# Mixer stage of a two-layer decoder trunk: its loads in one queue in order of use, no subtractions on GpSimd, another order of the first dense products

## The chip, the core and the metric

One core of a Trainium2 chip runs the whole trunk in one launch. The metric is the device time in microseconds of one execution. An execution is also profiled: its trace gives every instruction of the five engines (TensorE or PE with its weight loads PEld, VectorE or DVE, ScalarE or ACT, GpSimd or POOL, SyncE or SP), every DMA transfer, and the clock that TensorE was granted.

## What is computed

Two layers over 256 tokens of width 1024. Layer 0 is a causal pooling mixer and a dense SwiGLU, layer 1 a sparse attention and eight SwiGLU experts of which each token takes two. Each sub-layer ends in LayerNorm(ALPHA * x + f(x)). The change lies in the mixer and at the start of the dense layer:

```python
def pool_mixer(x, w_grp, scale):
    # four groups of 256 channels, windows 2, 4, 8, 16: running mean over the window, minus x
    ...
    y = jnp.einsum('bsgc,gcd->bsgd', pooled - xg, w_grp).reshape(B, S, D_MODEL)
    return y * scale

def swiglu(x, w_gu, w_down):
    g, u = jnp.split(x @ w_gu, 2, axis=-1)
    return (jax.nn.silu(g) * u) @ w_down

# layer 0
x = layer_norm(ALPHA * x + pool_mixer(x, pool_w, pool_scale), ln_g[0, 0], ln_b[0, 0])
x = layer_norm(ALPHA * x + swiglu(x, ffn_w_gu, ffn_w_down), ln_g[0, 1], ln_b[0, 1])
```

## The kernel before

**Numbers in two parts.** A float32 factor of the dense layer and of the attention's projections is split into a high part (ScalarE, a copy that rounds, line 154 for weights, 297 for activations) and a low part (VectorE or GpSimd, the difference, lines 164 and 300). A product is three matmuls: high by high, low by high, high by low. Weights come in units of 128 x 2048 floats (1 MB), in a fixed list; class `Units` walks it: `fetch` issues the DMA on SP's queue into one of four raw buffers (line 145) and the high copy, `low` makes the low part of the oldest unit that lacks it, on GpSimd if `pool=True`, and `take` hands out the pair. A raw buffer is free again when its low part is made.

**Mixer.** x lies as two halves of 128 tokens, `x0[:, 0]` and `x0[:, 1]`. `pooled(t, q)` multiplies x by constant window matrices `pc` (lines 398 and 400; the second half of the tokens needs both halves of x), ScalarE copies the result to `pT` (401), `mixed(t)` multiplies by the group weights `pw` into the banks `py` (407). VectorE scales `pw` by `pool_scale` (`scl`) first (413). `layer_norm` then runs on VectorE: per quarter of the channels a scaled sum and its statistics (240, 241), small steps on 128 x 1 values (254 to 263) with the two centrings by the gain among them (245), and the final scaling with the bias (277). TensorE transposes the result by the identity, which lies in `keep` (294), ScalarE takes the high part `xH`, VectorE the low part `xL`. The low parts of all four pieces are made after both halves are normalised (`lows`).

**What sets the order.** Every engine runs its instructions in the order in which the program writes them; the tile framework puts in the waits. SP's queue carries x, the matrices, `pw` and the weight units; GpSimd's queue carries `scl`, gain and bias `ln`, `keep` and `cst` (constants that the attention uses first). The first two weight units get their low parts from GpSimd, written behind the mixing and inside the loop over the halves; the third from VectorE behind the `lows`.

**First dense product.** `gate_up(0, ...)` (lines 440 to 461) multiplies unit 0 in three passes over 2 x 8 matmuls (447): high weights by `xH`, low weights by `xH`, high weights by `xL`. Its gate part `pg` stands in one of two banks with the tag `gu`, which the transposes of the second half of the tokens used last; its up part `pu` in one of four with the tag `acc`. Later products do the three matmuls in turn (223 to 225).

**After the front.** The dense layer has 22 such products and 11 down products, then the attention, then per expert 28 units of gate and up weights and 14 of down weights, whose DMAs run ahead as far as the raw buffers allow.

Of the kernel before, what the change touches and what calls it, by code (L numbers as in the profile page):

```python
# [12 lines left out]
BF16 = mybir.dt.bfloat16  # L13
# [6 lines left out]
P = 128  # L20
T = 256
D = 1024
KC = 8
# [20 lines left out]
_COLS = {}  # L44
# [138 lines left out]
def hybrid_trunk(ctx: ExitStack, tc: tile.TileContext, a, out):  # L183
    nc = tc.nc
# [11 lines left out]
    W = Units(nc, front.enter_context(tc.tile_pool(name="hlp", bufs=3)))  # L196
# [3 lines left out]
    nkeep = _COLS["upper"][0]  # L200
    keep = cp.tile([P, nkeep], F32, name="keep")
# [11 lines left out]
    def row(src, i=0):  # L213
        return bass.AP(tensor=src.tensor, offset=src.offset + i * D, ap=[[0, P], [1, D]])

    def ln_load(i, eng):
        t = lnp.tile([P, 2, D], F32, tag="ln", name=f"ln{i}")
        eng.dma_start(t[:, 0, :], row(a["ln_g"], i))
        eng.dma_start(t[:, 1, :], row(a["ln_b"], i))
        return t[:, 0, :], t[:, 1, :]  # L220
# [143 lines left out]
    with tc.tile_pool(name="psf", bufs=2, space=PSUM) as psf:  # L364
        def fbank(tag, name):
            return psf.tile([P, 512], F32, tag=tag, name=name, bufs={"tr": 2, "gu": 2, "acc": 4}[tag])


        x0 = actp.tile([P, 2, D], F32, tag="x", name="x0")
# [3 lines left out]
        with tc.tile_pool(name="poolp", bufs=1) as pp:  # L373
            at = _COLS["pool0"][0]
            pc = pp.tile([P, 3, 4, P], F32, name="pc")
            pw = pp.tile([P, 4, 2, 256], F32, name="pw")
            scl = pp.tile([P, D], F32, name="scl")
            pT = pp.tile([P, KC, T], F32, name="pT")
            nc.sync.dma_start(x0[:, 0, :], a["x"][:, 0, :])
            nc.sync.dma_start(pc[:, 0].rearrange("p g n -> p (g n)"), a["consts"][:, at:at + 512])  # L380
            nc.gpsimd.dma_start(scl, row(a["pool_scale"]))
            for h in range(2):
                nc.sync.dma_start(pw[:, 2 * h:2 * h + 2].rearrange("p g c d -> p (g c d)"),
                                  a["pool_w"][:, h * 1024:(h + 1) * 1024])
            nc.sync.dma_start(pc[:, 1:].rearrange("p k g n -> p (k g n)"), a["consts"][:, at + 512:])
            nc.sync.dma_start(x0[:, 1, :], a["x"][:, 1, :])
            gb = ln_load(0, nc.gpsimd)
            nc.gpsimd.dma_start(keep, a["consts"][:, :nkeep])
            nc.gpsimd.dma_start(cst, a["consts"][:, nkeep:at])
            py = [[fbank("acc", f"py{t}{n}") for n in range(2)] for t in range(2)]  # L390

            def pooled(t, q):
                pq = fbank("gu" if t else "tr", f"pool{t}{q}")
                for j in range(4):
                    c = 4 * q + j
                    ch = slice(c * P, (c + 1) * P)
                    o = pq[:, j * P:(j + 1) * P]
                    nc.tensor.matmul(o, x0[:, 0, ch], pc[:, t, c // 2, :], start=True, stop=t == 0)
                    if t:
                        nc.tensor.matmul(o, x0[:, 1, ch], pc[:, 2, c // 2, :], start=False, stop=True)  # L400
                nc.scalar.copy(pT[:, 4 * q:4 * q + 4, TS[t]], pq.rearrange("p (c n) -> p c n", n=P))

            def mixed(t):
                for n in range(2):
                    for g in range(2):
                        for c in range(2):
                            nc.tensor.matmul(py[t][n][:, g * 256:(g + 1) * 256], pT[:, 4 * n + 2 * g + c, TS[t]],
                                             pw[:, 2 * n + g, c, :], start=c == 0, stop=c == 1)

            pooled(0, 0)  # L410
            pooled(0, 1)
            for g in range(4):
                nc.vector.tensor_mul(pw[:, g], pw[:, g],
                                     scl[:, None, g * 256:(g + 1) * 256].to_broadcast([P, 2, 256]))
            mixed(0)
            pooled(1, 0)
            pooled(1, 1)
            mixed(1)
            W.fetch(1)
            W.low(1, pool=True)  # L420
            lows = []
            for t in range(2):
                def flips(q, t=t):
                    lows.append(transposed(x1[:, t, :], t, q, xH, xL, fbank("gu" if t else "tr", f"pt0{t}{q}"), True))

                layer_norm(x1[:, t, :], x0[:, t, :], py[t], gb, x1[:, t, :], f"0{t}", flips)
                W.fetch(1)
                if t == 0:
                    W.low(1, pool=True)
            for z in lows:  # L430
                z()
            W.low(1)


        gb = ln_load(1, nc.gpsimd)
        kp = nsa.enter_context(tc.tile_pool(name="nsak", bufs=1))
        with tc.tile_pool(name="ffnp", bufs=2) as fp:
            acc = []

            def gate_up(j, hH, hL, k):  # L440
                WH, WL = (w.rearrange("p (c u f) -> p c u f", c=KC, u=2) for w in W.take())
                if j == 0:
                    pg = [fbank("gu", "pg0"), fbank("acc", "pu0")]
                    for sz, mz in ((WH, xH), (WL, xH), (WH, xL)):
                        for u in range(2):
                            for c in range(KC):
                                nc.tensor.matmul(pg[u][:, :T], sz[:, c, u, :], mz[:, c, :], start=sz is WH and mz is xH
                                                 and c == 0, stop=mz is xL and c == KC - 1)
                    pg = [z[:, :T] for z in pg]
                else:  # L450
                    z = fbank("gu", f"pg{j}")
                    pg = [z[:, :T], z[:, T:]]
                    for u in range(2):
                        for c in range(KC):
                            mm3(pg[u], WH[:, c, u, :], WL[:, c, u, :], xH[:, c, :], xL[:, c, :], c == 0, c == KC - 1)
                s = fp.tile([P, T], F32, tag="sil", name=f"sil{j}")
                nc.scalar.activation(s, pg[0], AF.Silu)
                nc.vector.tensor_mul(s, s, pg[1])
                nc.scalar.activation(hH[:, k, :], s, AF.Copy)
                nc.vector.tensor_sub(hL[:, k, :], s, hH[:, k, :].bitcast(F32))  # L460
                W.ahead()

            def down(i, t, h, w):
                WH, WL = (z.rearrange("p (k n) -> p k n", k=2) for z in w)
                for k in range(2):
                    for n in range(2):
                        mm3(acc[t][n], h[0][:, k, TS[t]], h[1][:, k, TS[t]], WH[:, k, NS[n]], WL[:, k, NS[n]],
                            i == 0 and k == 0, i == ND - 1 and k == 1)

            hs = {}  # L470
            for i in range(ND):
                hs[i] = [fp.tile([P, 2, T], F32R, tag=f"h{z}", name=f"h{z}{i}", bufs=LAST + 1) for z in "HL"]
                for k in range(2):
                    gate_up(2 * i + k, *hs[i], k)
                if i == 1:
                    acc += [[fbank("acc", f"acc{t}{n}") for n in range(2)] for t in range(2)]
                if 0 <= i - 1 < ND - LAST:
                    w = W.take()
                    for t in range(2):
                        down(i - 1, t, hs[i - 1], w)  # L480
                    W.ahead()
            x2 = actp.tile([P, 2, D], F32, tag="x", name="x2")
            ws = {i: W.take("dn" if i == ND - LAST else None) for i in range(ND - LAST, ND)}
            for i in ws:
                down(i, 0, hs[i], ws[i])
            layer_norm(x2[:, 0, :], x1[:, 0, :], acc[0], gb, x2[:, 0, :], "10")
            for i in list(ws)[:-1]:
                down(i, 1, hs[i], ws[i])
            xH = actp.tile([P, KC, T], F32R, tag="xTH", name="xH1")
            xL = actp.tile([P, KC, T], F32R, tag="xTL", name="xL1")  # L490
            W.fetch(1)
            for q in range(2):
                transposed(x2[:, 0, :], 0, q, xH, xL, fbank("tr", f"pt10{q}"))
            W.low(1)
            down(ND - 1, 1, hs[ND - 1], ws[ND - 1])
            W.fetch(1)
            W.low(1)
            layer_norm(x2[:, 1, :], x1[:, 1, :], acc[1], gb, x2[:, 1, :], "11")
            W.fetch(1)
            W.low(1, pool=True)  # L500
# [1137 lines left out]
```

## Time and profile before

| | |
|---|---|
| median of three runs | 1255.92 us (1254.07 to 1257.68) |
| the profiled execution | 1254.77 us, span 1252.7 us |
| PE busy | 1184.8 us, 95% of the span, 7327 instructions |
| DVE, ACT, POOL busy | 361.3, 271.4, 30.2 us |
| HBM read | 412.25 MB, 330 GB/s over the span |

The span is what the trace covers; the profiled execution's own time is 2.1 us longer. Times in the trace count from the span's start. A busy TensorE is not one at its peak: its matmuls are pipelined and their ends modelled, so the pace is read from the starts or from counts in a stretch. A few records of matmuls can be missing. A plain float32 matmul leaves two records, one on the split parts leaves one.

### The profile page before, as it was taken

The page shows a single profiled execution, that of the slowest core. Times are in us where ns is not written, and L with a number is a line of the kernel's source. Part 1 is how long each engine was busy: PE and PEld are TensorE (multiplying, and loading weights), DVE is VectorE, ACT ScalarE, POOL GpSimd, SP SyncE. Part 2 cuts the span into 40 slices and gives each one's busy share as a digit, 9 for nine tenths or more (in the row PEclk, how much of TensorE's full clock was granted, in tenths as well). Part 3 has the DMA queues.
Part 4 walks back from the last instruction along what each step waited for, and adds up shares of the span by engine and source line. Part 5 has one row for each costly group of instructions (what it writes and reads, how often), then busy time and mean ns, then how long its engine had stood idle before and what let it go on. Part 6 is the DMA issues. An engine that isn't in the chain of part 4 may idle for free. (4 is left out here: it accounts for less than half of the span.)

```text
span 1252.7 us, 17577 instructions
## 1 busy us (share of the span) xinstructions
PE 1184.8 (95%) x7327; PEld 611.3 (49%) x7327; DVE 361.3 (29%) x638; ACT 271.4 (22%) x484; POOL 30.2 (2%) x36
## 2 busy tenths in 40 slices
PE   5899999998979999999999999999999999999983
PEld 4899999997757533333333343332343322334321
DVE  5545565755664510111010102001102001011204
ACT  2343553355562210110000011010011000010101
POOL 3000000200000000000000000000000000000001
PEclk9899999998889899999999999999999999999997
DMA  8455574332147899999999999999999999999993
GB/s 324 174 202 174 204 263 173 133 142 67 40 165 306 326 377 348 391 372 425 426 423 426 424 425 424 425 426 425 424 425 426 424 425 425 424 425 425 425 425 135
DMA packets 58805, 414.50 MB, mean 331 GB/s; under 512 B 6576, under 2 KB 6736, under 8 KB 9568
## 3 DMA queue, kind: packets, MB, share of 16 engines
q1 hardware_dynamic: 57168, 406.81, 80.1%
q0 software_dynamic: 1552, 6.51, 1.4%
q8 instruction: 59, 0.97, 0.3%
q14 instruction: 26, 0.21, 0.0%
HBM read 412.25 MB, written 1.05 MB: 330 GB/s over the span
## 5 line engine op out<-in xcount | busy, mean ns | idle before, releaser
L1343 PE MATMUL m<-raw,xe 128*64 128x512 f32 x1792 | 404.5, 599 | 2.0 <-DMA raw<-in_moe_gu_dram 1.9
L1343 PEld LDWEIGHTS m<-raw,xe 128*64 128x64 f32 x1792 | 121.5, 137 | 246.4 <-issue 233.0
L1394 PE MATMUL pd<-raw,hT 128*64 128x512 f32 x896 | 202.1, 595 | 6.4 <-DMA raw<-in_moe_dn_dram 5.7
L1365 DVE TENSOR_TENSOR h<-h,m 64x512 f32<-64x512 f32 x56 | 38.1, 680 | 483.9 <-ACT h L1364 483.9
L1364 ACT ACTIVATE h<-m 64x512 f32<-64x512 f32 x56 | 33.3, 594 | 469.1 <-PE m L1343 469.1
L1394 PEld LDWEIGHTS pd<-raw,hT 128*64 128x64 f32 x896 | 62.6, 137 | 139.6 <-issue 125.4
L164 DVE TENSOR_TENSOR wl<-raw,wh 128x2048 fp32r<-128x2048 f32 (+1 forms) x40 | 89.8, 2248 | 41.7 <-ACT wh L154 41.6
L223 PE MATMUL pg<-xH,wh 128*128 128x256 f32 x336 | 94.3, 281 | 0.0
L224 PE MATMUL pg<-xH,wl 128*128 128x256 f32 x336 | 94.3, 281 | 0.0
L225 PE MATMUL pg<-xL,wh 128*128 128x256 f32 x336 | 94.3, 281 | 0.0
L154 ACT ACTIVATE wh<-raw 128x2048 fp32r<-128x2048 f32 (+1 forms) x43 | 80.7, 1877 | 26.6 <-issue 23.7
L224 PEld LDWEIGHTS pg<-xH,wl 128*128 128x128 f32 x336 | 63.3, 189 | 0.3
L223 PEld LDWEIGHTS pg<-xH,wh 128*128 128x128 f32 x336 | 63.3, 189 | 0.3
L225 PEld LDWEIGHTS pg<-xL,wh 128*128 128x128 f32 x336 | 63.4, 189 | 0.0
L1379 ACT COPY hT<-fl 128x512 f32<-128x512 f32 (+1 forms) x32 | 17.1, 533 | 171.0 <-PE fl L1378 95.4
L1401 PE MATMUL pd<-raw,hT 128*32 128x512 f32 x448 | 52.2, 597 | 0.0
L1437 DVE SCALAR_TENSOR_TENSOR x<-cb,combP,x 128x512 f32<-128x512 f32 x24 | 17.5, 749 | 49.9 <-PE cb L1433 29.5
L223 PE MATMUL acc<-wh,hH 128*128 128x512 f32 x80 | 31.5, 393 | 0.0
L225 PE MATMUL acc<-wl,hH 128*128 128x512 f32 x80 | 31.4, 393 | 0.0
L224 PE MATMUL acc<-wh,hL 128*128 128x512 f32 x80 | 31.2, 390 | 0.0
L1401 PEld LDWEIGHTS pd<-raw,hT 128*32 128x32 f32 x448 | 12.5, 109 | 34.8 <-issue 30.1
L1385 DVE COPY hT<-fx 128x256 f32<-128x256 f32 (+1 forms) x16 | 6.2, 390 | 78.8 <-PE fx L1383 78.8
(421 smaller groups left out, 1290.0 us busy)
## 6 DMA issues: line engine op xcount, KB each, us to landing
raw<-in_moe_gu_dram SPq DMA_DIRECT2D x224, 1024.0 KB, 19.6
raw<-in_moe_dn_dram SPq DMA_DIRECT2D x111, 1024.0 KB, 19.6
raw<-in_ffn_gu_dram SPq DMA_DIRECT2D x22, 1024.0 KB, 4.9
raw<-in_ffn_dn_dram SPq DMA_DIRECT2D x11, 1024.0 KB, 4.8
raw<-in_nsa_in_dram SPq DMA_DIRECT2D x10, 1024.0 KB, 4.9
raw<-in_nsa_out_dram SPq DMA_DIRECT2D x4, 1024.0 KB, 4.9
w<-in_nsa_w_dram POOLq DMA_DIRECT2D x2, 1024.0 KB, 6.5
ln<-in_ln_g_dram POOLq DMA_DIRECT2D x3, 512.0 KB, 4.3
```

The costliest lines, as they stand in the source:

```text
L154: self.nc.scalar.activation(H[:, :n], raw[:, :n], AF.Copy)
L164: eng.tensor_sub(L[:, :n], raw[:, :n], H[:, :n].bitcast(F32))
L223: nc.tensor.matmul(outp, sH, mH, start=start, stop=False)
L224: nc.tensor.matmul(outp, sL, mH, start=False, stop=False)
L225: nc.tensor.matmul(outp, sH, mL, start=False, stop=stop)
L1343: nc.tensor.matmul(pa[b][g * SMALL:(g + 1) * SMALL, :], xs, w[:, i:i + 512], start=c == 0, stop=c == KC - 1)
L1364: nc.scalar.activation(s, pa[b][SMALL:, :], AF.Silu)
L1365: nc.vector.tensor_mul(s, s, pa[b][:SMALL, :])
L1379: nc.scalar.copy(hT[:, :nj, EXT:], pt[:, :nj * SMALL].rearrange("p (c n) -> p c n", n=SMALL))
L1394: nc.tensor.matmul(pd[0][n * SMALL:(n + 1) * SMALL, :], hT[:, j, EXT:], w[:, at + n * 512:at + (n + 1) * 512], start=G == 0 and j == 0, st ...
L1401: nc.tensor.matmul(pd[1][k * EXT:(k + 1) * EXT, :], hT[:, j, :EXT], w[:, at + n * 512:at + (n + 1) * 512], start=G == 0 and j < 2, stop=G ...
L1437: nc.vector.scalar_tensor_tensor(yacc[:, t, NS[n]], pt, (combP if p else comb)[:, t, p:p + 1], yacc[:, t, NS[n]], op0=ALU.mult, op1=ALU.add)
```

## The change

In the mixer, SP's queue gets the second half of x ahead of the rest of `pc`, and then gain, bias and `keep`, which were on GpSimd's queue; `cst` goes behind layer 0's second gain and bias on GpSimd's queue. VectorE fills a tile `zero`, and nine matmuls of it into an unused bank are written ahead of the first pooling. The two subtractions on GpSimd go; all three low parts of weights are written behind the `lows`, on VectorE. The first dense product has both parts in `acc` banks, and its second pass takes `xL`, the third the low weights.

```diff
--- before.py
+++ after.py
@@ -377,16 +377,21 @@
             scl = pp.tile([P, D], F32, name="scl")
             pT = pp.tile([P, KC, T], F32, name="pT")
             nc.sync.dma_start(x0[:, 0, :], a["x"][:, 0, :])
+            nc.gpsimd.dma_start(scl, row(a["pool_scale"]))
             nc.sync.dma_start(pc[:, 0].rearrange("p g n -> p (g n)"), a["consts"][:, at:at + 512])
-            nc.gpsimd.dma_start(scl, row(a["pool_scale"]))
             for h in range(2):
                 nc.sync.dma_start(pw[:, 2 * h:2 * h + 2].rearrange("p g c d -> p (g c d)"),
                                   a["pool_w"][:, h * 1024:(h + 1) * 1024])
+            nc.sync.dma_start(x0[:, 1, :], a["x"][:, 1, :])
             nc.sync.dma_start(pc[:, 1:].rearrange("p k g n -> p (k g n)"), a["consts"][:, at + 512:])
-            nc.sync.dma_start(x0[:, 1, :], a["x"][:, 1, :])
-            gb = ln_load(0, nc.gpsimd)
-            nc.gpsimd.dma_start(keep, a["consts"][:, :nkeep])
-            nc.gpsimd.dma_start(cst, a["consts"][:, nkeep:at])
+            gb = ln_load(0, nc.sync)
+            nc.sync.dma_start(keep, a["consts"][:, :nkeep])
+
+            zero = pp.tile([P, 512], BF16, name="zero")
+            nc.vector.memset(zero, 0.0)
+            idle = fbank("gu", "idle")
+            for _ in range(9):
+                nc.tensor.matmul(idle, zero[:, :P], zero, start=True, stop=True)
             py = [[fbank("acc", f"py{t}{n}") for n in range(2)] for t in range(2)]
 
             def pooled(t, q):
@@ -417,7 +422,6 @@
             pooled(1, 1)
             mixed(1)
             W.fetch(1)
-            W.low(1, pool=True)
             lows = []
             for t in range(2):
                 def flips(q, t=t):
@@ -425,14 +429,13 @@
 
                 layer_norm(x1[:, t, :], x0[:, t, :], py[t], gb, x1[:, t, :], f"0{t}", flips)
                 W.fetch(1)
-                if t == 0:
-                    W.low(1, pool=True)
             for z in lows:
                 z()
-            W.low(1)
+            W.low(3)
 
 
         gb = ln_load(1, nc.gpsimd)
+        nc.gpsimd.dma_start(cst, a["consts"][:, nkeep:_COLS["pool0"][0]])
         kp = nsa.enter_context(tc.tile_pool(name="nsak", bufs=1))
         with tc.tile_pool(name="ffnp", bufs=2) as fp:
             acc = []
@@ -440,12 +443,12 @@
             def gate_up(j, hH, hL, k):
                 WH, WL = (w.rearrange("p (c u f) -> p c u f", c=KC, u=2) for w in W.take())
                 if j == 0:
-                    pg = [fbank("gu", "pg0"), fbank("acc", "pu0")]
-                    for sz, mz in ((WH, xH), (WL, xH), (WH, xL)):
+                    pg = [fbank("acc", "pg0"), fbank("acc", "pu0")]
+                    for sz, mz in ((WH, xH), (WH, xL), (WL, xH)):
                         for u in range(2):
                             for c in range(KC):
                                 nc.tensor.matmul(pg[u][:, :T], sz[:, c, u, :], mz[:, c, :], start=sz is WH and mz is xH
-                                                 and c == 0, stop=mz is xL and c == KC - 1)
+                                                 and c == 0, stop=sz is WL and c == KC - 1)
                     pg = [z[:, :T] for z in pg]
                 else:
                     z = fbank("gu", f"pg{j}")
```

SP's queue at the program's start, before (x_86 is x, ln_104 gain and bias of the first normalisation, raw the weight units; in brackets what the instruction waits for, DMAHW being transfers of SP's queue):

```order
L379 DMA x_86<-in_x_dram 128x1024
L380 DMA pc<-in_consts_dram 128x512
L383 DMA pw<-in_pool_w_dram 128x1024 x2
L385 DMA pc<-in_consts_dram 128x1024
L386 DMA x_86<-in_x_dram 128x1024
L145 DMA raw_165<-in_ffn_gu_dram 128x2048
L145 DMA raw_210<-in_ffn_gu_dram 128x2048
L145 DMA raw_255<-in_ffn_gu_dram 128x2048 [waits DMAHW0_49]
L145 DMA raw_332<-in_ffn_gu_dram 128x2048 [waits DMAHW1_49]
```

and now:

```order
L379 DMA x_86<-in_x_dram 128x1024
L381 DMA pc<-in_consts_dram 128x512
L383 DMA pw<-in_pool_w_dram 128x1024 x2
L385 DMA x_86<-in_x_dram 128x1024
L386 DMA pc<-in_consts_dram 128x1024
L218 DMA ln_104<-in_ln_g_dram 128x1024
L219 DMA ln_104<-in_ln_b_dram 128x1024
L388 DMA keep<-in_consts_dram 128x472 [waits DMAHW0_49]
L145 DMA raw_176<-in_ffn_gu_dram 128x2048 [waits DMAHW1_49]
L145 DMA raw_220<-in_ffn_gu_dram 128x2048 [waits DMAHW2_49]
L145 DMA raw_264<-in_ffn_gu_dram 128x2048 [waits DMAHW3_49]
L145 DMA raw_344<-in_ffn_gu_dram 128x2048 [waits DMAHW4_49]
```

Gain, bias and `keep` now stand ahead of the first weight unit, and two more of the listed transfers wait for an earlier one to land.

VectorE from the end of the second half's normalisation, before (xL the low parts of the activations, wl of weights, sil and hL the gate's results):

```order
L277 SCALAR_TENSOR_TENSOR x_87<-x_87,y_01_225,ln_104 128x512 x2
L300 TENSOR_TENSOR xL_89<-pt_197,xH_88 128x4x128
L300 TENSOR_TENSOR xL_89<-pt_204,xH_88 128x4x128
L300 TENSOR_TENSOR xL_89<-pt_242,xH_88 128x4x128
L300 TENSOR_TENSOR xL_89<-pt_249,xH_88 128x4x128
L164 TENSOR_TENSOR wl_258<-raw_255,wh_257 128x2048
L458 TENSOR_TENSOR sil_327<-sil_327,pu_278 128x256
L460 TENSOR_TENSOR hL_276<-sil_327,hH_275 128x256
```

and now:

```order
L277 SCALAR_TENSOR_TENSOR x_87<-x_87,y_01_234,ln_104 128x512 x2
L300 TENSOR_TENSOR xL_89<-pt_207,xH_88 128x4x128
L300 TENSOR_TENSOR xL_89<-pt_214,xH_88 128x4x128
L300 TENSOR_TENSOR xL_89<-pt_251,xH_88 128x4x128
L300 TENSOR_TENSOR xL_89<-pt_258,xH_88 128x4x128
L164 TENSOR_TENSOR wl_179<-raw_176,wh_178 128x2048
L164 TENSOR_TENSOR wl_223<-raw_220,wh_222 128x2048
L164 TENSOR_TENSOR wl_267<-raw_264,wh_266 128x2048
L461 TENSOR_TENSOR sil_339<-sil_339,pu_290 128x256
L463 TENSOR_TENSOR hL_288<-sil_339,hH_287 128x256
```

Three subtractions of weights stand between the activations' low parts and the first result of the gate, where one stood.

TensorE at the last transposes and the first dense product, before (pg and pu its two banks, wh and wl the weights' parts):

```order
L294 MATMUL pt_249<-keep,x_87 128x128 [waits DVE_49,PE_49]
L294 MATMUL pt_249<-keep,x_87 128x128 x3
L447 MATMUL pg_277<-xH_88,wh_167 128x256 [waits DVE_49]
L447 MATMUL pg_277<-xH_88,wh_167 128x256 x3
L447 MATMUL pg_277<-xH_88,wh_167 128x256 [waits Activation_49]
L447 MATMUL pg_277<-xH_88,wh_167 128x256 x3
L447 MATMUL pu_278<-xH_88,wh_167 128x256 x8
L447 MATMUL pg_277<-xH_88,wl_168 128x256 [waits Pool_49]
L447 MATMUL pg_277<-xH_88,wl_168 128x256 x7
L447 MATMUL pu_278<-xH_88,wl_168 128x256 x8
L447 MATMUL pg_277<-xL_89,wh_167 128x256 x4
L447 MATMUL pg_277<-xL_89,wh_167 128x256 [waits DVE_49]
```

and now:

```order
L294 MATMUL pt_258<-keep,x_87 128x128 [waits DVE_49,PE_49]
L294 MATMUL pt_258<-keep,x_87 128x128 x3
L450 MATMUL pg_289<-xH_88,wh_178 128x256 [waits Activation_49]
L450 MATMUL pg_289<-xH_88,wh_178 128x256 x3
L450 MATMUL pg_289<-xH_88,wh_178 128x256 [waits Activation_49]
L450 MATMUL pg_289<-xH_88,wh_178 128x256 x3
L450 MATMUL pu_290<-xH_88,wh_178 128x256 x8
L450 MATMUL pg_289<-xL_89,wh_178 128x256 [waits DVE_49]
L450 MATMUL pg_289<-xL_89,wh_178 128x256 x3
L450 MATMUL pg_289<-xL_89,wh_178 128x256 [waits DVE_49]
L450 MATMUL pg_289<-xL_89,wh_178 128x256 x3
L450 MATMUL pu_290<-xL_89,wh_178 128x256 x8
```

The first matmul waited for VectorE, which had to leave the bank, and waits only for ScalarE's high part now; the low parts of the activations come in the second pass, and GpSimd is not waited for.

## Rows read from the trace of the kernel before

**Rows 1.** The page's slices: busy share of the DMA engines in 40 equal slices of the span, in tenths.

```profile
DMA  8455574332147899999999999999999999999993
```

**Rows 2.** Stretches by engine. Columns: the stretch and its length, busy time (instructions) of PE, PEld, DVE, ACT and POOL, the mean granted clock of TensorE (1.00 is 2.4 GHz, 0.50 is 1.2), share of the DMA engines, GB/s.

```profile
5.00:10.00 5.00, 3.48 (x16) 3.32 (x16) 0.00 (x0) 0.70 (x2) 0.00 (x0) 1.00 1.01 401
...
25.00:30.00 5.00, 0.00 (x0) 0.00 (x0) 4.86 (x6) 2.41 (x3) 5.00 (x2) 0.99 0.33 107
29.50:30.00 0.50, 0.00 (x0) 0.00 (x0) 0.50 (x1) 0.00 (x0) 0.50 (x1) 0.90 0.78 328
...
43.50:44.00 0.50, 0.50 (x6) 0.50 (x6) 0.00 (x0) 0.00 (x0) 0.00 (x0) 0.95 0.44 164
45.00:50.00 5.00, 5.00 (x45) 5.00 (x44) 1.90 (x3) 2.61 (x3) 0.00 (x0) 1.00 0.16 69
290.00:295.00 5.00, 1.88 (x14) 1.76 (x16) 2.50 (x5) 3.97 (x16) 0.00 (x0) 0.77 0.00 0
...
350.00:355.00 5.00, 3.17 (x8) 2.48 (x8) 2.83 (x9) 5.00 (x19) 0.00 (x0) 0.58 0.00 0
...
425.00:430.00 5.00, 5.00 (x36) 1.45 (x36) 3.55 (x19) 1.57 (x2) 0.00 (x0) 0.92 0.11 18
```

**Rows 3.** Instructions in order of time, 6 to 21 us. Columns: start, length, engine, line, operation with output and inputs, count; in brackets the engine's idle time before and what ended it.

```profile
6.37 3.48 PE L398 MATMUL pool<-pc,x 128*128 128x128 f32 x16 [6.37 <-DMA pc<-in_consts_dram]
...
10.01 1.29 DVE L413 TENSOR_TENSOR pw<-pw,scl 128x512 f32<-128x512 f32 x2 [10.01 <-DMA pw<-in_pool_w_dram]
...
12.43 1.29 DVE L413 TENSOR_TENSOR pw<-pw,scl 128x512 f32<-128x512 f32 x2 [1.13 <-DMA pw<-in_pool_w_dram]
...
13.22 1.97 PE L407 MATMUL py<-pw,pT 128*128 128x256 f32 x8 [0.46 <-DVE pw L413]
...
15.94 0.69 DVE L241 BATCH_NORM_STATS2 stats<-x 128x6 f32<-128x512 f32 x1
...
16.98 0.49 PE L400 MATMUL pool<-pc,x 128*128 128x128 f32 x2 [1.29 <-DMA x<-in_x_dram]
...
17.31 0.39 PE L398 MATMUL pool<-pc,x 128*128 128x128 f32 x2
...
17.43 0.75 DVE L245 SCALAR_TENSOR_TENSOR x<-x,mv,ln 128x512 f32<-128x512 f32 x1
17.53 0.39 PE L400 MATMUL pool<-pc,x 128*128 128x128 f32 x2
...
19.65 1.42 DVE L277 SCALAR_TENSOR_TENSOR x<-x,y,ln 128x512 f32<-128x512 f32 x2
...
20.44 3.62 PE L407 MATMUL py<-pw,pT 128*128 128x256 f32 x16
```

**Rows 4.** The same, 23 to 46 us.

```profile
23.12 8.97 POOL L164 TENSOR_TENSOR wl<-raw,wh 128x2048 fp32r<-128x2048 f32 x2 [19.02 <-ACT wh L154]
...
23.89 1.04 PE L294 MATMUL pt<-keep,x 128*128 128x128 f32 x8
...
24.82 0.69 DVE L241 BATCH_NORM_STATS2 stats<-x 128x6 f32<-128x512 f32 x1
...
26.17 1.49 DVE L260 SCALAR_TENSOR_TENSOR w<-y,v 128x1 f32<-128x1 f32 x1
27.58 5.06 DVE L245 SCALAR_TENSOR_TENSOR x<-x,mv,ln 128x512 f32<-128x512 f32 x1
...
34.12 1.41 DVE L277 SCALAR_TENSOR_TENSOR x<-x,y,ln 128x512 f32<-128x512 f32 x2
...
35.02 1.94 PE L294 MATMUL pt<-keep,x 128*128 128x128 f32 x8 [10.09 <-DVE x L277]
...
37.00 0.60 ACT L297 ACTIVATE xH<-pt 128x512 fp32r<-128x512 f32 x1 [0.26 <-PE pt L294]
...
37.52 2.08 PE L447 MATMUL pg<-xH,wh 128*128 128x256 f32 x8 [0.56 <-DVE xL L300]
...
39.42 2.29 DVE L164 TENSOR_TENSOR wl<-raw,wh 128x2048 fp32r<-128x2048 f32 x1 [1.11 <-ACT wh L154]
...
45.97 0.28 PE L223 MATMUL pg<-xH,wh 128*128 128x256 f32 x1
```

**Rows 5.** DMA over the first 40 us: GB/s in 40 slices of 1 us, then transfers by kind, with the queue that issued them, their count, the size of each and the median time from issue to landing.

```profile
GB/s 0 41 180 260 264 401 414 414 373 401 422 402 426 408 416 418 438 418 434 401 451 410 434 410 426 213 0 0 66 254 434 295 0 131 442 442 49 229 365 332
...
pw<-in_pool_w_dram SPq DMA_DIRECT2D x2, 512.0 KB, 9.3
ln<-in_ln_g_dram POOLq DMA_DIRECT2D x2, 512.0 KB, 6.9
...
scl<-in_pool_scale_dram POOLq DMA_DIRECT2D x1, 512.0 KB, 7.6
...
keep<-in_consts_dram POOLq DMA_DIRECT2D x1, 236.0 KB, 12.0
```

**Rows 6.** Waits of TensorE over the whole span: total us, times, longest.

```profile
PE pd L1394 <- DMA raw<-in_moe_dn_dram: 5.7, 9, 1.4
PE out L223 <- DVE rt L556: 3.4, 1, 3.4
PE qt L597 <- DVE kcT L697: 3.3, 1, 3.3
```

## The prediction

> **What bounds the kernel now.** I read the page's slices first, then the stretches by engine, then the first 46 us in order of time. The slices show the DMA engines loaded lightly in the first third of the span and at 9 tenths or more behind it [rows 1]. In the stretches TensorE is busy without a gap once the dense layer runs: 5.00 of 5.00 us with 45 matmuls, 0.111 us each [rows 2]. The first dense product starts at 37.52 [rows 4]. Until then TensorE mostly waits; from 25 to 30 it does nothing at all [rows 2]. So a microsecond by which the product at 37.52 comes earlier is a microsecond off the end, as long as nothing behind it was waiting for something that does not move. Nothing seems to be: in the dense layer TensorE is the bound, and in the expert layers its waits for weights sum to only 5.7 us for the down-projections [rows 6]; at 425 to 430 the DMA engines are at a share of 0.11, so the weight stream had filled its buffers and waited for TensorE [rows 2].
>
> Why 37.52? The normalisation of the second half of the tokens ends at 34.12 + 1.41 = 35.53, on VectorE [rows 4]. The same chain of small steps took, for the first half, from the end of its statistics at 15.94 + 0.69 = 16.63 to 19.65 + 1.42 = 21.07, which is 4.44 us [rows 3]. For the second half it runs from 24.82 + 0.69 = 25.51 to 35.53, which is 10.02 us. The excess stands in two rows: a 128x1 step of 1.49 us and a centring of 5.06 us that took 0.75 us before, both while GpSimd subtracts, from 23.12 for 8.97 us [rows 3, 4]. VectorE is waiting for GpSimd.
>
> **The change, part by part.**
>
> *Subtractions off GpSimd.* Two subtractions leave GpSimd, and no other GpSimd work lies in that stretch. The second half's chain then costs what the first half's did: 10.02 - 4.44 = **5.58 us** gained.
>
> *Load order.* Before, GpSimd's queue moves scl, gain, bias, keep and cst (2.2 MB) side by side with SP's. The sizes show the split: by 10.0 us, when the first half of pw has landed, the rates of each microsecond sum to 2.75 MB, of which SP's queue up to that transfer is only 1.31 MB [rows 3, 5]. By 16.98, when the second half of x lands, they sum to 5.7 MB, where SP's 2.88 and GpSimd's 2.2 make 5.1; some 0.5 MB of the following transfers is always under way. After the change only scl (0.52 MB) stands beside SP's queue. With the same curve of rates and the same 0.5 MB on top, my estimates are: first half of pw at 8.95 (2.33 MB), second at 10.3 (before 12.43), second half of x at 11.6 (before 16.98), the rest of pc at 12.8, gain 14.1, bias 15.4, keep 16.0. scl landed at 1.26 + 7.6 = 8.9 and stays [rows 5].
>
> VectorE's scaling of pw, 1.29 us a half [rows 3], is then done at 10.3 and 11.7. TensorE ends the first pooling at 6.37 + 3.48 = 9.85 and mixes the first half of the tokens in two runs of about 1.8 us each, to 13.5 (before 13.22 + 1.97 = 15.19) [rows 3]. Statistics of the first half end at 15.0 (before 16.63), its normalisation at 19.45. Then VectorE goes straight to the second half: two quarters, each a scaled sum and a statistics step of about 0.7 us (the last of them 0.69 [rows 4]), to 22.4 instead of 25.51: **3.1 us** gained. TensorE keeps up with that: pooling of the second half 13.5 to 17.1 (32 records at 0.111, two records of a pair every 0.22 [rows 3]), mixing 3.62 us to 20.8, just when VectorE wants the last quarter. So both engines set the end there. Gain is wanted 0.8 us after the statistics, at 15.9, bias at 18.1: 1.8 and 2.7 us to spare. The bounds: if pw came no earlier than now, 1.5 us of the 3.1 are lost, since the second pooling need not wait for x any more; if everything landed at once, TensorE's 9.85 + 3.65 still stands, and little more is won.
>
> SP's queue has new waits. The ninth transfer on it, keep, waits for the first, x, to land (6.3 us), and the four raw units behind it for pc, pw, pw and x (to 11.6). Behind each waiting issue the queue still holds over 1 MB to move, so the engines do not run dry, and raw unit 0 lands at about 18.4 by the same curve, ahead of its turn on ScalarE and VectorE. On GpSimd, cst is queued behind the next gain and bias, which wait for the second normalisation; only the attention reads it, behind the whole dense layer, so this costs nothing.
>
> *Nine idle matmuls.* They wait for one fill of 128 partitions on VectorE and stand ahead of the first pooling on TensorE. A matmul of 512 columns takes at most 0.46 us (twice what 256 columns take at the lower clock, worked out below), so they last 2 to 4.2 us, from about 1.2; x is there at 6.37. Cost 0. What they bring: the granted clock over 5 to 10 us reads 1.00 [rows 2], yet the 16 records of the first pooling take 0.217 us each, where the same 128x128 records of the second take 0.111 [rows 3]. By the pace the first pooling ran at 1.2 GHz and all behind it at 2.4. The Trainium skill (TensorE: Matmul & The Clock Gate, "What's actually happening") says that the throttled clock is the default and activity releases it; the pace agrees, the clock column does not. By that rule the idle matmuls could halve the pooling's 3.48 us, by the column they do nothing. I take 0, since the mixing behind it waits for pw, scaled at 9.65 at the earliest, so at most 0.2 us could be won.
>
> *Banks and pass order.* Before, pg sits in a bank that VectorE is still reading for the low parts, and the product starts at 37.52, although TensorE's transposes ended at 35.02 + 1.94 = 36.96 [rows 4]. In an acc bank it starts at once on the chunks that are there; the last copy (0.60 us) lands while four matmuls of 0.23 run. **0.54 us** gained. The low parts of x are now wanted one pass after the start.
>
> *VectorE's new load.* Three subtractions of 2.29 us [rows 4] stand in its line behind the low parts. With normalisation ended at E, the low parts are done at E + 2.8 (as now: 39.42 less 1.11 idle, less 35.53), the units at E + 5.1, 7.4 and 9.7. TensorE starts at E + 1.45. The first product took 45.97 - 37.52 = 8.45 us for 48 matmuls [rows 4]. The clock rose at 43.5 [rows 2]; the 2.45 us behind that hold 22 of them at 0.111, so 26 took 6.0 us, 0.23 each, and a pass of 16 takes 3.7 us at the lower clock. It wants unit 0 at E + 8.8 and unit 1 at E + 9.9: 3.7 and 2.5 us to spare. The raw buffers come back at 32 to 37 instead of 27.6 to 41.7, and the fifth unit is wanted only after two more products. Nothing lost.
>
> *The clock in the gap.* It fell at about 29.95, 5 us into the idle stretch, and rose at 43.5 [rows 2]. After the change TensorE idles from 21.9 (transposes of the first half, 1.04 us [rows 4]) to 26.2: 4.3 us. Later waits of 3.3 and 3.4 us [rows 6] left the stretches that hold their ends at a mean of 0.77 and 0.58 [rows 2]. So 4.3 us is enough, and the first product again begins at the lower clock. Nothing gained or lost.
>
> **Sum.** 5.58 + 3.1 + 0.54 = 9.2 us. The profiled execution took 1254.77 (span 1252.7), so 1245.6; the median of the runs, 1255.92, lies 1.15 above it, so **1246.7 us**. E moves from 35.53 to 26.9, the product from 37.52 to 28.3.
>
> **Rivals.**
>
> *The clock stays up in the shorter gap.* Then the first product takes 48 x 0.111 = 5.3 instead of 8.45, the last transposes 0.45 less, and unit 1 comes 0.35 late: 3.2 us more, 1243.5. For it: 4.3 us of idling instead of 10. Against it: the two shorter waits. 12%.
>
> *The front stays cold or the loads come no sooner.* If the clock rises only during the mixing, its 3.62 us can double; if pw lands as now, 1.5 us go. Both move the two chains together: 1.5 to 3.6 us given back, 1248.2 to 1250.3, I say 1248.7. For it: the first pooling did run slowly, and the idle matmuls end a microsecond or more before x lands. Against it: before, one pooling was enough to raise the clock. 18%.
>
> *The front is hidden.* If the expert weights, not TensorE, set the end from a start that does not move, nothing comes of it: 1255.9. Against it stand the share of 0.11 and the small waits for weights. 4%.
>
> *Slower: a starved first product keeps the clock down.* VectorE's subtractions now lie between the passes. If TensorE had to wait for each unit, the clock would not rise, and a product of 48 matmuls would take 48 x 0.23 = 11.0 instead of 5.3 us. The first would lose 2.6 more than now, each further one 5.7; two leave 0.9 of the 9.2 us, from three on it is slower: 2.6 + 2 x 5.7 - 9.2 = 4.8, or 1260.7. Against it: at the lower clock TensorE is the late one, by 2.5 us. 2%.
>
> **How the numbers follow.** My forecast has the remaining 64%. A measurement of this kernel can tell about 0.3%, 3.8 us. Forecast and the first two rivals are all faster than that, 94%; the hidden front is the same, 4%; the last is slower, 2%. The range runs from 1242.5 (the clock rival, with a microsecond of scatter; the three runs before lie 3.6 us apart) to 1250.3 (the worst of the cold front).
>
> **What would show it.** The second half's centring at 0.75 us and no GpSimd work before 200 us; the second half of x landing near 11.6; normalisation ending near 27 and the first product starting within 1.5 us of it; the clock low from about 27 to 34; no wait of TensorE for wl. I am wrong if the first product starts before 26 or after 31, or if the shift at 50 us is not there at the end.

## The result and the profile after

The changed kernel took 1242.23 us (median of five runs, 1239.79 to 1246.76) against 1255.92 (five runs): a ratio of 0.9902, with an interval of 0.9874 to 0.9929, so 12.3 us faster by the ratio, 8.9 to 15.8 by the interval. Timed once more it stood at 0.9909 (0.9894 to 0.9924), 11.4 us, or 9.5 to 13.3. The forecast was 9.2 us, 1246.7 in a range of 1242.5 to 1250.3: the second timing's median, 1244.12, lies in it, the first's lies 0.3 us below its lower end. The profiled execution took 1244.38 us (span 1242.6), 10.4 less than the one before.

The front of the kernel after, in order of time (columns as in [rows 3]; line 403 is the pooling, 412 the mixing, 418 the scaling of pw, 450 the first dense product, 394 the idle matmuls, 223 the start of the second product):

```profile
1.20 4.02 PE L394 MATMUL idle<-zero 128*128 128x512 bf16 x9 [1.20 <-DVE zero L391]
...
6.16 3.75 PE L403 MATMUL pool<-pc,x 128*128 128x128 f32 x16 [0.94 <-DMA pc<-in_consts_dram]
...
8.99 2.50 DVE L418 TENSOR_TENSOR pw<-pw,scl 128x512 f32<-128x512 f32 x4 [7.84 <-DMA pw<-in_pool_w_dram]
...
9.78 3.88 PE L412 MATMUL py<-pw,pT 128*128 128x256 f32 x16
...
14.42 0.69 DVE L241 BATCH_NORM_STATS2 stats<-x 128x6 f32<-128x512 f32 x1
...
17.07 3.62 PE L412 MATMUL py<-pw,pT 128*128 128x256 f32 x16
...
18.13 1.42 DVE L277 SCALAR_TENSOR_TENSOR x<-x,y,ln 128x512 f32<-128x512 f32 x2
...
21.49 0.69 DVE L241 BATCH_NORM_STATS2 stats<-x 128x6 f32<-128x512 f32 x1
...
22.84 0.22 DVE L260 SCALAR_TENSOR_TENSOR w<-y,v 128x1 f32<-128x1 f32 x1
22.98 0.75 DVE L245 SCALAR_TENSOR_TENSOR x<-x,mv,ln 128x512 f32<-128x512 f32 x1
...
25.20 1.42 DVE L277 SCALAR_TENSOR_TENSOR x<-x,y,ln 128x512 f32<-128x512 f32 x2
...
26.10 1.94 PE L294 MATMUL pt<-keep,x 128*128 128x128 f32 x8 [4.54 <-DVE x L277]
...
27.88 2.07 PE L450 MATMUL pg<-xH,wh 128*128 128x256 f32 x8
...
29.32 6.68 DVE L164 TENSOR_TENSOR wl<-raw,wh 128x2048 fp32r<-128x2048 f32 x3
...
34.90 0.28 PE L223 MATMUL pg<-xH,wh 128*128 128x256 f32 x1
```

Compare this with [rows 3, 4]. The second half's chain, from the end of the statistics at 21.49 + 0.69 = 22.18 to 25.20 + 1.42 = 26.62, takes 4.44 us instead of 10.02, to the digit what the first half takes; the step of 1.49 us is 0.22, the centring of 5.06 us is 0.75. Mixing of the first half runs from 9.78 through to 13.66, where it ended at 15.19, and the second pooling follows without waiting for x. The first product starts at 27.88, 1.26 us after the normalisation (before 1.99), 9.6 us earlier than at 37.52. The second product starts at 34.90 instead of 45.97, 11.1 us earlier.

The loads of the first 40 us (columns as in [rows 5]):

```profile
GB/s 0 41 168 274 289 412 414 369 414 422 422 426 406 355 303 436 451 426 418 426 442 426 418 418 287 33 0 16 205 315 311 282 345 300 442 352 401 393 262 344
...
pw<-in_pool_w_dram SPq DMA_DIRECT2D x2, 512.0 KB, 7.6
...
scl<-in_pool_scale_dram POOLq DMA_DIRECT2D x1, 512.0 KB, 7.4
...
ln<-in_ln_g_dram SPq DMA_DIRECT2D x1, 512.0 KB, 10.2
ln<-in_ln_b_dram SPq DMA_DIRECT2D x1, 512.0 KB, 11.2
...
keep<-in_consts_dram SPq DMA_DIRECT2D x1, 236.0 KB, 10.7
```

Gain lands at 3.74 + 10.2 = 13.9, bias at 4.33 + 11.2 = 15.5, keep at 5.46 + 10.7 = 16.2 (the issues are at 3.74, 4.33 and 5.46); pw is there at 8.99. The estimates were 14.1, 15.4, 16.0 and 8.95. The second half of x, issued at 2.60, lands 8.8 us later, at 11.4 (estimate 11.6). Five of SP's listed transfers now wait for an earlier one, where two did; even so ScalarE has raw unit 0 at 18.67 (estimate 18.4).

The clock around the gap (columns as in [rows 2]):

```profile
23.50:24.00 0.50, 0.00 (x0) 0.00 (x0) 0.45 (x3) 0.50 (x1) 0.00 (x0) 0.81 0.97 410
25.00:30.00 5.00, 3.90 (x18) 3.69 (x19) 4.76 (x8) 2.52 (x3) 1.58 (x3) 0.50 0.37 114
30.50:31.00 0.50, 0.50 (x6) 0.50 (x6) 0.50 (x1) 0.50 (x1) 0.00 (x0) 0.86 0.96 344
```

It fell at about 23.8, 2.2 us into the idle stretch, and rose at 30.6, 2.8 us after the first product had begun; before, it fell 5 us into the stretch and rose 6.0 us after the product's start.

Where does the time go behind the front? Three marks in each profiled execution: the start of the second product, the last transposes of the dense layer's result (line 294), and the first expert matmul.

```
                      normal-   first    second   dense layer's  first    span
                      isation   product  product  transposes     expert
                      ends                                       matmul
before                35.53     37.52    45.97    236.52         422.48   1252.7
after                 26.62     27.88    34.90    225.58         412.26   1242.6
after, again          26.78     28.04    35.59    226.31         410.97   1241.6
e1 subs on GpSimd     33.75     35.00    42.75    233.48         418.30   1248.0
e2 loads back         29.94     31.19    38.68    229.16         416.58   1247.5
e3 bank back          27.10     29.09    36.55    227.06         414.39   1245.5
e4 no idle            26.86     28.13    35.21    225.72         410.10   1239.9
e5 gap fill           26.85     27.65    33.64    224.20         409.99   1239.9
e10 gap fill, again   26.73     27.53    33.52    224.25         411.14   1241.7
e6 only subs          29.97     31.95    40.08    230.58         416.25   1246.7
e7 only loads         33.51     35.49    43.52    234.29         421.97   1252.7
e8 passes back        26.23     27.48    35.17    225.86         411.67   1241.8
```

From the second product to the transposes every execution takes 190.5 to 190.8 us, and from the first expert matmul to the end 829.7 to 831.1. Through both of these stretches the front's gain is carried whole. Between the two, in the attention and the routing, it is 184.4 to 187.7 us, without regard to the front: that is the scatter of 3 us in which differences of a microsecond drown.

### The profile page after: what moved, and what is told of

Its sections match the earlier page's. It is cut to its first block, busy times and chain, and to the rows that moved or that the text cites. A ratio compares the mean times of both kernels' runs of the same rounds, so it can differ in the third digit from the quotient of the medians.

```text
span 1242.6 us, 17596 instructions
## 1 busy us (share of the span) xinstructions
PE 1188.5 (96%) x7336; PEld 612.6 (49%) x7336; DVE 360.0 (29%) x641; ACT 271.2 (22%) x484; POOL 18.6 (1%) x31
## 5 line engine op out<-in xcount | busy, mean ns | idle before, releaser
L164 DVE TENSOR_TENSOR wl<-raw,wh 128x2048 fp32r<-128x2048 f32 (+1 forms) x42 | 94.2, 2249 | 40.6 <-ACT wh L154 40.5
```

The source lines that it names most:

```text
L164: eng.tensor_sub(L[:, :n], raw[:, :n], H[:, :n].bitcast(F32))
```

## The experiments

**The subtractions back on GpSimd.**

```diff
             W.fetch(1)
+            W.low(1, pool=True)
             lows = []
...
                 W.fetch(1)
+                if t == 0:
+                    W.low(1, pool=True)
             for z in lows:
                 z()
-            W.low(3)
+            W.low(1)
```

> The changed kernel, with the first two subtractions of weights back on GpSimd where they were. Theory (a VectorE step with both inputs in SBUF waits for the GpSimd subtraction that is running): they now run from about 20.6 to 29.6 us, the second half's normalisation waits through most of that, and ends near 33 us instead of 26.6; the first dense product starts near 34.3 instead of 27.9, and the time is about 6 us above the changed kernel's (1244.4 in its profiled execution), near 1250. Rival (the gain came from the loads, GpSimd cost nothing): normalisation still ends at 26.6 to 27, the time stays within 1 us.

Its front (line 453 is the first product):

```profile
21.34 8.96 POOL L164 TENSOR_TENSOR wl<-raw,wh 128x2048 fp32r<-128x2048 f32 x2 [19.36 <-ACT wh L154]
21.44 0.69 DVE L241 BATCH_NORM_STATS2 stats<-x 128x6 f32<-128x512 f32 x1
...
22.79 3.07 DVE L260 SCALAR_TENSOR_TENSOR w<-y,v 128x1 f32<-128x1 f32 x1
25.79 5.07 DVE L245 SCALAR_TENSOR_TENSOR x<-x,mv,ln 128x512 f32<-128x512 f32 x1
...
32.33 1.42 DVE L277 SCALAR_TENSOR_TENSOR x<-x,y,ln 128x512 f32<-128x512 f32 x2
...
35.00 2.08 PE L453 MATMUL pg<-xH,wh 128*128 128x256 f32 x8
```

Normalisation ends at 33.75, the product starts at 35.00, the time is 1250.09 us, a ratio to the kernel before of 0.9944 (0.9926 to 0.9963). The theory holds to 0.8 us. The rows show the kind of wait too. GpSimd's two subtractions run from 21.34 to 30.30, the first to about 25.8 (21.34 + 8.96 / 2). The statistics step, with one input, takes its usual 0.69 beside it. The small step of two inputs in SBUF begins at 22.79 and ends at 25.86, when the first subtraction does; the centring ends at 30.86, 0.56 after the second. So VectorE seems not to be slowed down but to stand still until the running GpSimd instruction is over: in the kernel before and with the loads alone, too, the small step ends within 0.1 us of the first subtraction's end and the centring 0.55 us after the second's. The Trainium skill (SBUF — State Buffer, "Who interferes with whom") says so: a VectorE instruction with two SBUF inputs contends with a GpSimd instruction that reads SBUF, whichever issues first keeps the shared ports for the whole instruction, and a VectorE instruction with at most one SBUF input, outside the modes that use both pairs of ports, does not contend. The trace agrees, with 3.07 against 0.22 us and 5.07 against 0.75.

**The loads back in their old order.**

```diff
-            nc.sync.dma_start(x0[:, 1, :], a["x"][:, 1, :])
             nc.sync.dma_start(pc[:, 1:].rearrange("p k g n -> p (k g n)"), a["consts"][:, at + 512:])
-            gb = ln_load(0, nc.sync)
-            nc.sync.dma_start(keep, a["consts"][:, :nkeep])
+            nc.sync.dma_start(x0[:, 1, :], a["x"][:, 1, :])
+            gb = ln_load(0, nc.gpsimd)
+            nc.gpsimd.dma_start(keep, a["consts"][:, :nkeep])
+            nc.gpsimd.dma_start(cst, a["consts"][:, nkeep:at])
```

> The changed kernel, with the loads in their old order and queues. Theory (the old order makes the second pooling wait for x until 17 us): second half's statistics end at 25.5 instead of 22.2, normalisation at 29.9 instead of 26.6, first dense product near 31.2, time about 3.3 us above the changed kernel's, near 1247.7. Rival (VectorE alone sets the front, the loads only move slack about): normalisation ends at 27 to 28, at most 1.5 us lost.

```profile
16.98 0.49 PE L406 MATMUL pool<-pc,x 128*128 128x128 f32 x2 [1.00 <-DMA x<-in_x_dram]
...
24.81 0.69 DVE L241 BATCH_NORM_STATS2 stats<-x 128x6 f32<-128x512 f32 x1
...
28.52 1.42 DVE L277 SCALAR_TENSOR_TENSOR x<-x,y,ln 128x512 f32<-128x512 f32 x2
...
31.19 2.07 PE L450 MATMUL pg<-xH,wh 128*128 128x256 f32 x8
```

The second pooling waits for x until 16.98 again, the statistics end at 25.50, normalisation at 29.94, the product starts at 31.19: 3.3 us later than in the changed kernel, as expected. 1248.56 us (near 1247.7 was expected), ratio 0.9931 (0.9911 to 0.995).

**Without the idle matmuls.**

```diff
-            zero = pp.tile([P, 512], BF16, name="zero")
-            nc.vector.memset(zero, 0.0)
-            idle = fbank("gu", "idle")
-            for _ in range(9):
-                nc.tensor.matmul(idle, zero[:, :P], zero, start=True, stop=True)
```

> The changed kernel without the nine idle matmuls and the fill. Theory (they end before the first pooling and do not raise the clock for it): first pooling at 0.22 to 0.23 us a record as now, mixing of the first half starts at 9.7 to 9.9, first dense product at 27.9 within 0.5 us, unless the clock is still low during the mixing. Rival (they raise the clock in time for the mixing): without them the first mixing's 16 records take up to 7.3 instead of 3.9 us, and the first dense product starts 1 to 3.6 us later.

```profile
6.13 3.75 PE L398 MATMUL pool<-pc,x 128*128 128x128 f32 x16 [6.13 <-DMA pc<-in_consts_dram]
...
9.82 4.09 PE L407 MATMUL py<-pw,pT 128*128 128x256 f32 x16
...
25.45 1.41 DVE L277 SCALAR_TENSOR_TENSOR x<-x,y,ln 128x512 f32<-128x512 f32 x2
```

The product starts at 28.13, 0.25 us later than in the first trace of the changed kernel and 0.1 later than in the second; 1244.73 us, ratio 0.991 (0.9894 to 0.9927). So they bring nothing that can be seen. It is not that they never raise the clock: in the gap-fill kernel below, the first pooling's 16 records take 2.02 us instead of 3.75, and so they do in five more of the traces with idle matmuls. But the mixing starts at 9.6 to 10.4 in all of them, because pw, scaled, is not there sooner.

**The clock held through the gap.**

```diff
                 W.fetch(1)
+                if t == 0:
+                    idle = fbank("acc", "idle2")
+                    for _ in range(18):
+                        nc.tensor.matmul(idle, zero[:, :P], zero, start=True, stop=True)
```

> The changed kernel, with 18 more idle matmuls (128x512, bf16, into the bank of py00) on TensorE between the transposes of the two halves, where it idles from 21.6 to 26.1 us. Theory (the idle stretch alone drops the clock): at 0.22 us each they end at 25.5, the clock stays at 1.00, the last transposes take 1.0 instead of 1.9 us, the first dense product 5.3 to 5.7 instead of 7.0, the second product starts near 32.5 instead of 34.9, and the time is 2 to 2.5 us below the changed kernel's. Rival (idle matmuls do not hold the clock, as those at the start did not raise it): the clock falls at some point before 27, the matmuls stretch to 0.43 us and the transposes start late, 0 to 3 us lost.

Its front (435 the new idle matmuls, 454 the first product):

```profile
6.24 2.02 PE L403 MATMUL pool<-pc,x 128*128 128x128 f32 x16 [1.59 <-DMA pc<-in_consts_dram]
...
9.87 3.69 PE L412 MATMUL py<-pw,pT 128*128 128x256 f32 x16 [1.60 <-DVE pw L418]
...
21.68 4.05 PE L435 MATMUL idle<-zero 128*128 128x512 bf16 x17
...
26.33 1.29 PE L294 MATMUL pt<-keep,x 128*128 128x128 f32 x8 [0.61 <-DVE x L277]
...
27.65 1.41 PE L454 MATMUL pg<-xH,wh 128*128 128x256 f32 x8
...
33.64 0.28 PE L223 MATMUL pg<-xH,wh 128*128 128x256 f32 x1
```

The granted clock is 1.00 through the first 40 us; the first product takes 33.64 - 27.65 = 6.0 us instead of 7.0, the second starts 1.3 us earlier than in the changed kernel. That is about half of what was expected (5.3 to 5.7 us, and 32.5). The time does not show it: 1243.25 us, ratio 0.9898 (0.9881 to 0.9914). So it was run beside the changed kernel on one chip:

> The changed kernel once more, to weigh the gain of 9.2 us that the trace's terms sum to against the 12.3 us (8.9 to 15.8) of the first timing. Theory (the terms are the gain, the rest is the clock's luck in single executions): 9 to 11 us, a ratio of 0.991 to 0.993. Rival (something behind the front gains as well): 12 us or more again, a ratio of 0.9904 or less.

> The changed kernel with 18 idle matmuls in the gap between the transposes, beside the changed kernel on the same chip. Theory (the clock held through the gap brings the second product 1.3 us earlier than in the changed kernel's first trace, and up to 3 us where the clock there rises late): 1 to 2.5 us below the changed kernel's median. Rival (the attention's stretches at the lower clock swamp it): within 1 us of it.

The changed kernel: 1244.12 us, ratio 0.9909 (0.9894 to 0.9924). These 11.4 us lie between the theory (9 to 11) and the rival (12 or more), and the interval reaches into both, so the run does not decide between them. With the gap filled: 1244.99 us, 0.9918 (0.9904 to 0.9931). Its second product starts 2.1 us earlier (33.52 against 35.59), but in these two executions its attention and routing took 186.9 us against 184.7. So the rival's "within 1 us" came true: the gain that was expected of the gap fill is not there, and no version that beats the changed kernel is shown. Whether the front's gain is lost by chance or by rule in the attention stays open.

**Only the subtractions, and only the loads, on the kernel before.** The first has the edit of the first experiment the other way round, the second that of the second experiment the other way round, with cst behind the next gain and bias.

> The kernel before, with nothing changed but the first two subtractions of weights, which go from GpSimd to VectorE behind the activations' low parts. Theory (GpSimd's subtractions cost 5.6 us of waiting on VectorE by themselves): second half's statistics end at 25.5 as before, normalisation at 29.9 to 30.0 instead of 35.5, first dense product starts near 31.9, unit 0's low part (35.1) is just there for the second pass, time 5 to 6 us below the kernel before. Rival (the wait is only uncovered together with the earlier loads): normalisation ends after 33, at most 2 us gained.

```profile
24.84 0.69 DVE L241 BATCH_NORM_STATS2 stats<-x 128x6 f32<-128x512 f32 x1
...
28.55 1.42 DVE L277 SCALAR_TENSOR_TENSOR x<-x,y,ln 128x512 f32<-128x512 f32 x2
...
31.95 2.08 PE L444 MATMUL pg<-xH,wh 128*128 128x256 f32 x8 [0.56 <-DVE xL L300]
```

Normalisation ends at 29.97, 5.56 us earlier than before, the product starts at 31.95, the time is 1249.99 us, ratio 0.9961 (0.9948 to 0.9974): 3.3 to 6.5 us.

> The kernel before, with nothing changed but the order and queues of the loads. Theory (VectorE cannot end the normalisation before GpSimd has ended its two subtractions, which start when ScalarE has made unit 0's high part, near 21): statistics of the second half end near 22.2, but normalisation only near 33.7, first dense product near 35.7, time about 2 us below the kernel before: less than the 3.1 us that this term has in the sum. Rival (the terms add): normalisation ends at 32.4 or earlier, 3 us or more gained.

```profile
19.11 1.91 ACT L154 ACTIVATE wh<-raw 128x2048 fp32r<-128x2048 f32 x1 [1.47 <-DMA raw<-in_ffn_gu_dram]
...
21.11 8.95 POOL L164 TENSOR_TENSOR wl<-raw,wh 128x2048 fp32r<-128x2048 f32 x2 [19.13 <-ACT wh L154]
21.27 0.69 DVE L241 BATCH_NORM_STATS2 stats<-x 128x6 f32<-128x512 f32 x1
...
32.09 1.42 DVE L277 SCALAR_TENSOR_TENSOR x<-x,y,ln 128x512 f32<-128x512 f32 x2
...
35.49 2.08 PE L447 MATMUL pg<-xH,wh 128*128 128x256 f32 x8 [0.56 <-DVE xL L300]
```

The statistics end at 21.96, 3.55 us earlier than before, but GpSimd subtracts from 21.11 to 30.06, and normalisation ends only at 33.51, 2.0 us earlier. 1252.7 us, ratio 0.9986 (0.9975 to 0.9998): 0.3 to 3.1 us. By the end of the normalisation the two parts alone gain 5.56 and 2.02, together 8.9. Earlier loads alone leave VectorE waiting longer for GpSimd (11.55 us from statistics to end instead of 10.02), since the subtractions start when ScalarE has made the high part. That moves from 23.12 to 21.11, 2.0 us earlier, because ScalarE now waits for raw unit 0 to land; the normalisation's end moves by the same 2.0 us.

**The bank, and the order of the passes, back.**

```diff
-                    pg = [fbank("acc", "pg0"), fbank("acc", "pu0")]
+                    pg = [fbank("gu", "pg0"), fbank("acc", "pu0")]
```

> The changed kernel with the gate part of the first dense product back in the gu bank. Theory (the bank is given back only by the third low part on VectorE): the first dense product starts 1.9 to 2.0 us after the normalisation's end instead of 1.25, so 0.6 to 0.7 us later. Rival (it waits for ScalarE's high part anyway): no difference over 0.1 us.

```profile
25.69 1.41 DVE L277 SCALAR_TENSOR_TENSOR x<-x,y,ln 128x512 f32<-128x512 f32 x2
...
29.09 2.07 PE L450 MATMUL pg<-xH,wh 128*128 128x256 f32 x8 [0.56 <-DVE xL L300]
```

1.99 us from the normalisation's end to the product instead of 1.26, and the wait is for the low part xL, as before: 0.73 us. This and the next experiment are one execution each; their differences in total time say nothing.

```diff
-                    for sz, mz in ((WH, xH), (WH, xL), (WL, xH)):
+                    for sz, mz in ((WH, xH), (WL, xH), (WH, xL)):
```

> The changed kernel with the first dense product's passes in their old order (low weights second). Theory (unit 0's low part is ready 2.2 us after the last low part of the activations, near 31.6): TensorE, at the lower clock, wants it 3.2 to 3.7 us after its start, near 31.1 to 31.6, so it waits at most 0.5 us, and the order of the passes is worth at most that. Rival (the order is what keeps TensorE fed): a wait of over 1 us between the first and the second pass.

```profile
27.48 2.08 PE L450 MATMUL pg<-xH,wh 128*128 128x256 f32 x8
...
31.26 1.22 PE L450 MATMUL pg<-xH,wl 128*128 128x256 f32 x8 [0.46 <-DVE wl L164]
```

One wait of 0.46 us for the low weights between the first and the second pass, and no other.

## Why the prediction came out as it did

- **GpSimd off VectorE's back, 5.58 us.** Right: the chain went from 10.02 to 4.44, and alone it moves the normalisation's end by 5.56. Beside the earlier loads it is worth more: with the subtractions back on GpSimd the end comes 7.1 us later (33.75 against 26.62). Either order of taking the two parts gives 8.9 us, 5.56 and then 3.3 or 2.0 and then 7.1.
- **Loads, 3.1 us.** Right in size: the statistics end 3.3 us earlier (25.51 to 22.18), and putting the loads back costs 3.3. The sum of bytes ahead of a transfer, at the rates of the trace before and with half a megabyte under way, put the four landings above right to 0.2 us. That TensorE and VectorE set the end together held too: the mixing ended at 20.69, the last quarter's sum began at 20.79. The term holds only with GpSimd out of the way: the loads alone gain 2.0 by the normalisation's end.
- **Bank, 0.54 us.** 0.73 by the experiment. The 0.54 was read from the modelled end of the last transposes, which lies behind the true start of what follows (now 26.10 + 1.94 = 28.04, while the product starts at 27.88). The order of the passes had no price of its own in the sum; in the one execution without it TensorE waits 0.46 us for the low weights.
- **Idle matmuls, nothing.** Right. The first pooling takes 2.02 us in six of the eight traces with idle matmuls and 3.5 to 3.75 in all others; this changes no time, because the mixing waits for pw. The Trainium skill (TensorE: Matmul & The Clock Gate, "What's actually happening") says that the throttled clock is the default and that activity releases it. The pace agrees in those six; in the other two the pace stayed low behind nine idle matmuls, and the clock column reads 1.00 either way.
- **VectorE's new load, nothing lost.** Right: its three subtractions end at 36.0, and TensorE goes from the first to the second product without a wait.
- **The clock in the gap, "nothing gained or lost".** This is the term that was mis-sized. That it would fall was right, and so the first rival fell. But its times were wrong: it was low from 23.8 to 30.6, not from about 27 to 34. And the price of the lower clock was taken from one execution, in which the first product took 8.45 us. It took 7.0 and 7.6 in the two traces of the changed kernel; 0.9 to 1.4 us of the gain come from that. Whether this is chance is not shown. In the ten traces in which the clock fell, the product took 8.0, 8.1 and 8.45 us in the three with the old bank, the old order of passes and no idle matmuls, and 7.0 to 7.75 in the seven others. That speaks for an effect of the change; but with any one of these three parts taken back the product stayed at 7.1 to 7.7, so no run shows which of them it would be.

So in the two traces of the changed kernel the gain is 8.8 to 8.9 us by the normalisation's end, 0.7 more by the product's start and 0.9 to 1.4 more by its end: 10.4 and 11.1 us at the start of the second product, against 9.2 in the sum. Both timed intervals hold these, and the sum's 9.2 lies in the first and 0.3 us short of the second. A part of the first timing's 12.3 us that goes beyond them is not traced to a place; the attention's scatter is large enough for it. The cold front, the hidden front and the starved product did not come: the first mixing took 3.7 to 3.9 us in the two traces, the front's gain stands at the end, and TensorE waits for no low weights.

## What to carry to other kernels

Before giving a slack engine work beside VectorE, ask what VectorE runs meanwhile: here a chain of small steps, some with two inputs in SBUF, waited out each running GpSimd subtraction, so two subtractions of 4.5 us on an engine with nothing else to do cost 5.6 us on the critical path. Order loads by first use in one queue, and forecast each landing by the bytes ahead of it at the rate that the trace shows. Gains of parts that meet in one wait don't add when taken one by one, so price them together; and take the price of a state that comes and goes, such as a lower clock, from more than one execution.

## What was not expected of the hardware

The same stretch of attention and routing took 184.4 to 187.7 us in twelve executions whose instructions there are the same, whatever the front did. The front's own clock differed as well: the first pooling's 16 records took 2.02 us in some traces with idle matmuls and 3.7 in others. In the ten traces without the gap fill the granted clock fell 2.1 to 5.0 us into the idle stretch between the transposes of the two halves. And a clock that idle matmuls held at 2.4 GHz through the gap, 1.3 to 2.1 us at the second product, left no mark on the time.
